# A bias table through 16 copies and 8 skewed loads, a spread scale row, and another opening order

## Chip, cores, metric

The kernel runs on one core of one Trainium2 chip. The metric is the device time of one execution in microseconds (us); of several runs the median counts. Lower is better.

## What is computed

Two layers of a decoder block on 256 rows of width 1024, all in float32. Cut to what matters here:

```python
def hybrid_layer(x, rel_bias, norm1_g, w_in, ...):
    h = rms_norm(x, norm1_g)                 # rows scaled by norm1_g
    z = h @ w_in                             # columns for retention, conv, gMLP, window attention, gates
    ...
    yd = swa_attention(zd, swa_q_g, swa_k_g, swa_sinks, rel_bias)
    ...
    x = x + mix @ w_out                      # mix: the four branches, gated and summed
    h = rms_norm(x, norm2_g)
    return x + swiglu(h)

def swa_attention(...):                      # blocks of 128 rows, window 128, 8 heads
    s = q @ k.T * d ** -0.5
    bias = rel_bias[t5_bucket(dist)]         # a function of the distance and the head alone
    s = where(valid, s + bias, -inf)
    p = softmax with one sink per head
```

The bias of a head depends on the distance alone. So a table of 384 values per head, read with a shift of one place per query row, gives the 128 x 256 block of biases.

## The kernel before

**Tiles.** The 256 rows are two tiles of 128 (t = 0, 1). Weights stream from HBM in units of 1 MB; a unit is two halves of 512 KB (`raw`, 6 buffers). Each half is split in two float32r parts: ScalarE (ACT) rounds it to `wh` (`part`, L117), VectorE (DVE) subtracts to get `wl` (L118); there are 8 buffers of each. A product is three matmuls (`mm`, L140 to L142): xh·wh, xh·wl, xl·wh. Every half gives 12 such matmuls over the two tiles.

**Order of the work in a layer.** `columns` takes the window attention's q columns (4 halves), its k and v columns (2 halves), then, as chunks of 4 halves, the conv input `pa`, the conv gate `pg`, retention q, k, v, gate, and the gMLP. The window attention is a generator (`swa_task`): transposes of q and k (`swa_qkT`) fall due after `pa`, scores and row maxima (`swa_soft`, with the bias added on DVE at L375) after `pg`, the exponentials follow on ACT (L389, L395). Gates, branches, output projection and FFN follow.

**Who sets the order.** Except in the opening, which is written out by hand on TensorE (PE), ACT and DVE, a scheduler places the instructions of each engine. All loads of weights are issued by the SyncE queue (SPq), in order, and so are nearly all other transfers: what waits in that queue holds back every load behind it. Each engine, too, works strictly in its own order.

**Opening and norm.** `opening` loads tile 0 of x, the scale row of the first norm spread to 128 partitions (`load_norm`, L223, 512 KB), and the first 4 halves. PE runs warm-up matmuls on a tile of zeros. `norm` squares and sums on ACT (L198), takes the root on GpSimd (`rsqrt`, L184), scales on DVE (L207); PE transposes, and `split` (ACT L174, DVE L176) makes the two parts of h.

**Bias table.** `constants` builds it, called after the q, k and v columns: a matmul (L281) of the 32 x 8 `rel_bias` with a 32 x 384 table of ones and zeros (`hot`) gives 8 rows of 384; DVE adds the mask (`jm`, L283); one transfer (L285) writes each of the 8 rows 128 times to DRAM (`rd`, 8 x 128 x 384), and one load (L288) reads it back with a row step of 383 elements, so that each partition is shifted by one.

Of the kernel before, what the change touches and what calls it, by code (L numbers as in the profile page):

```python
# [16 lines left out]
P = 128  # L17
D = 1024
# [13 lines left out]
LEAD = 96  # L32
C_QG, C_KG, C_CB, C_LG, C_LB, C_GB, C_SK, C_CW = 0, 1, 2, 6, 10, 14, 18, 26
# [47 lines left out]
class Kernel:  # L81
# [110 lines left out]
    def norm(self, t, raw=False):  # L192
        nc = self.nc
        x, g = self.x[t], self.ng
        ms = self.small("ms")
        hn = [self.work("hn") for _ in range(2)]
        for n in range(2):
            nc.scalar.activation(  # L198
                hn[n], x[:, n * 512 : (n + 1) * 512], AF.Square, scale=1.0 / 32.0, accum_out=ms[:, n : n + 1]
            )  # L200
# [4 lines left out]
        for n in range(2):  # L205
            s = slice(n * 512, (n + 1) * 512)
            nc.vector.scalar_tensor_tensor(  # L207
                out=hn[n], in0=x[:, s], scalar=ms[:, 3:4], in1=g[:, s], op0=ALU.mult, op1=ALU.mult
            )
# [16 lines left out]
    def setup(self):  # L226
# [3 lines left out]
        self.nhalf = self.lead.tile([P, LEAD], F32, name="nhalf")  # L230
        nc.gpsimd.memset(self.nhalf, -0.5)
# [3 lines left out]
    def opening(self):  # L235
        nc, a, pin = self.nc, self.a, self.tc.keep_in_program_order
        self.setup()
        for n in range(2):
            c = slice(n * 512, (n + 1) * 512)
            pin(nc.sync.dma_start(out=self.x[0][:, c], in_=a["x"][0:P, c]))  # L240
        nc.scalar.dma_start(out=self.ident, in_=a["ident"])
        self.ng = self.load_norm(0, 0)
# [3 lines left out]
        self.warm = self.wk.tile([P, W], BF16, tag="wk", name="warm")  # L246
        EN = mybir.EngineType
        with self.tc.manual_schedule(engines={EN.PE, EN.Activation, EN.DVE}):
            nc.vector.memset(self.warm, 0.0)
            self.warm_up(14)  # L250
            hn = self.norm(0, raw=True)
            ps = [self.transpose4(hn[n]) for n in range(2)]
            self.warm_up(3)
            h0 = self.act_tile(0)
            nc.vector.tensor_copy(first[0][0], first[0][2])
            self.split(h0, 0, ps[0], 1.0)
            nc.vector.tensor_tensor(
                out=first[0][1], in0=first[0][2], in1=first[0][0].bitcast(F32), op=ALU.subtract
            )
            self.split(h0, 4, ps[1], 1.0)  # L260
            for half in first[1:]:
                self.part(*half)
        return h0
# [5 lines left out]

    def constants(self):  # L270
        nc, cp, a = self.nc, self.cp, self.a
        c = cp.tile([P, NCONST], F32, name="const")
        self.const = c
        rel = cp.tile([32, 8], F32, name="rel")
        hot = self.wk.tile([32, 384], F32, tag="wk", name="hot")
        jm = self.wk.tile([8, 384], F32, tag="wk", name="jm")
        nc.sync.dma_start(out=rel, in_=a["rel_bias"])
        nc.sync.dma_start(out=hot, in_=a["hot"])
        nc.sync.dma_start(out=jm, in_=a["jmask"])
        ps = self.bank()  # L280
        nc.tensor.matmul(ps[:8, :384], rel, hot, start=True, stop=True)  # L281
        r8 = self.wk.tile([8, 384], F32, tag="wk", name="r8")
        nc.vector.tensor_tensor(out=r8, in0=ps[:8, :384], in1=jm, op=ALU.add)  # L283
# [650 lines left out]
def shape_constants():  # L934
# [26 lines left out]
    jmask = np.tile(np.where(valid, 0.0, NEG).astype(np.float32)[None], (8, 1))  # L961
    return const, hot, jmask, np.eye(P, dtype=np.float32)
# [47 lines left out]
```

## Time and profile before

| what | value |
|---|---|
| median of 3 runs | 980.57 us (980.22 to 982.9) |
| the profiled execution's own time | 982.4 us |
| its span in the profile | 980.3 us |
| busy: PE, DVE, ACT, POOL | 956.2, 681.7, 482.5, 38.7 us |
| HBM read, mean | 175.46 MB, 182 GB/s |

The span is the time from the first to the last instruction that the profiler recorded; the execution's own time is a little longer than that. PE is busy nearly all the time, but a busy share is an average over stages: the 24 us in which PE has nothing to do lie mostly in two places, at the start and some 60 us in. Busy time of PE also holds matmuls that run at the lower of TensorE's two clock levels; the granted clock (PEclk, 1.00 is 2.4 GHz, 0.50 is 1.2 GHz) shows where.

### The profile page before, as it was taken

The page shows a single profiled execution, that of the slowest core. Times are in us where ns is not written, and L with a number is a line of the kernel's source. Part 1 is how long each engine was busy: PE and PEld are TensorE (multiplying, and loading weights), DVE is VectorE, ACT ScalarE, POOL GpSimd, SP SyncE. Part 2 cuts the span into 40 slices and gives each one's busy share as a digit, 9 for nine tenths or more (in the row PEclk, how much of TensorE's full clock was granted, in tenths as well). Part 3 has the DMA queues.
Part 4 walks back from the last instruction along what each step waited for, and adds up shares of the span by engine and source line. Part 5 has one row for each costly group of instructions (what it writes and reads, how often), then busy time and mean ns, then how long its engine had stood idle before and what let it go on. Part 6 is the DMA issues. An engine that isn't in the chain of part 4 may idle for free.

```text
span 980.3 us, 12353 instructions
## 1 busy us (share of the span) xinstructions
PE 956.2 (98%) x4567; PEld 789.3 (81%) x4567; DVE 681.7 (70%) x1051; ACT 482.5 (49%) x688; POOL 38.7 (4%) x38
## 2 busy tenths in 40 slices
PE   8959999999999999999999999999999999999998
PEld 5846788888888888888988778888888888888887
DVE  6507999999767655556566699999866676555552
ACT  5407846454555444444455774644446455444440
POOL 0200001100000000000001000100010000000000
PEclk9988999999999999999999999999999999999999
DMA  9558564665654665655555246466656357656521
GB/s 350 169 79 294 172 231 160 226 198 180 199 166 154 213 221 183 196 184 183 190 171 210 91 155 212 129 192 194 194 176 193 105 191 244 203 177 194 190 89 43
DMA packets 51060, 178.89 MB, mean 182 GB/s; under 512 B 5520, under 2 KB 7992, under 8 KB 50872
## 3 DMA queue, kind: packets, MB, share of 16 engines
q1 hardware_dynamic: 50856, 178.04, 56.1%
q8 instruction: 36, 0.59, 0.2%
q14 instruction: 24, 0.20, 0.1%
q10 hardware_dynamic: 144, 0.07, 0.0%
HBM read 175.46 MB, written 2.62 MB: 182 GB/s over the span
## 4 chain that ended last, share of the span: by engine, by line
PE 90%; DMA 4%; ACT 3%; DVE 2%; issue 1%; SPq 0%; POOL 0%; ACTq 0%; DVEq 0%
PE acc L141 20%; PE acc L142 20%; PE acc L140 20%; PE mid L140 8%; PE mid L142 8%; PE mid L141 8%; DMA raw<-wu 3%; PE mid L167 2%; ACT sc L389 1%; PE mid L817 1%; ACT sc L395 1%; DVE wl L118 1%; DMA ng<-norms 1%; ACT wh L117 0%; PE mid L588 0%
## 5 line engine op out<-in xcount | busy, mean ns | idle before, releaser
L118 DVE TENSOR_TENSOR wl<-raw,wh 128x1024 fp32r<-128x1024 f32 x319 | 385.2, 1223 | 183.4 <-ACT wh L117 178.8
L117 ACT CAST wh<-raw 128x1024 fp32r<-128x1024 f32 x319 | 332.2, 1055 | 314.0 <-PE acc L142 163.7
L140 PE MATMUL acc<-wh,hT 128*128 128x512 f32 (+1 forms) x640 | 250.5, 392 | 13.7 <-ACT wh L117 13.7
L141 PE MATMUL acc<-wl,hT 128*128 128x512 f32 (+1 forms) x640 | 248.0, 387 | 1.0 <-DVE wl L118 0.9
L142 PE MATMUL acc<-wh,hT 128*128 128x512 f32 (+1 forms) x640 | 247.9, 387 | 0.0
L140 PEld LDWEIGHTS acc<-wh,hT 128*128 128x128 f32 x640 | 121.1, 189 | 37.4 <-ACT wh L117 14.1
L140 PE MATMUL mid<-wh,hT 128*128 128x512 f32 (+1 forms) x384 | 143.7, 374 | 0.0
L142 PE MATMUL mid<-wh,hT 128*128 128x512 f32 (+1 forms) x384 | 142.7, 372 | 0.0
L141 PEld LDWEIGHTS acc<-wl,hT 128*128 128x128 f32 x640 | 121.1, 189 | 26.8 <-DVE wl L118 2.8
L141 PE MATMUL mid<-wl,hT 128*128 128x512 f32 (+1 forms) x384 | 142.6, 371 | 0.0
L142 PEld LDWEIGHTS acc<-wh,hT 128*128 128x128 f32 x640 | 120.7, 189 | 25.3 <-issue 0.6
L140 PE MATMUL acc<-wh,yT 128*128 128x512 f32 x304 | 119.1, 392 | 0.0
L141 PE MATMUL acc<-wl,yT 128*128 128x512 f32 x304 | 118.4, 389 | 0.0
L142 PE MATMUL acc<-wh,yT 128*128 128x512 f32 x304 | 118.1, 389 | 0.0
L446 DVE SCALAR_TENSOR_TENSOR ca<-uT,col,ca 128x256 f32<-128x256 f32 x240 | 101.8, 486 | 3.4 <-ACT ca L440 3.3
L142 PEld LDWEIGHTS mid<-wh,hT 128*128 128x128 f32 x384 | 72.3, 188 | 12.6
L140 PEld LDWEIGHTS mid<-wh,hT 128*128 128x128 f32 x384 | 72.3, 188 | 12.2
L141 PEld LDWEIGHTS mid<-wl,hT 128*128 128x128 f32 x384 | 72.4, 188 | 12.2
L142 PEld LDWEIGHTS acc<-wh,yT 128*128 128x128 f32 x304 | 57.1, 188 | 12.2 <-DVE yT L821 0.3
L140 PEld LDWEIGHTS acc<-wh,yT 128*128 128x128 f32 x304 | 57.1, 188 | 11.8 <-ACT yT L820 0.4
L141 PEld LDWEIGHTS acc<-wl,yT 128*128 128x128 f32 x304 | 57.1, 188 | 11.5
L740 ACT ACTIVATE gth<-acc 128x512 f32<-128x512 f32 x32 | 19.2, 599 | 30.9 <-PE acc L142 30.9
(141 smaller groups left out, 590.8 us busy)
## 6 DMA issues: line engine op xcount, KB each, us to landing
raw<-wu SPq DMA_DIRECT2D x320, 512.0 KB, 4.2
ng<-norms SPq DMA_DIRECT2D x4, 512.0 KB, 5.7
rows<-rows SPq DMA_DIRECT2D x2, 768.0 KB, 6.3
rd<-r SPq DMA_DIRECT2D x1, 1536.0 KB
const<-const SPq DMA_DIRECT2D x1, 1088.0 KB, 6.8
bias<-rd SPq DMA_DIRECT2D x1, 1024.0 KB, 5.7
out<-x SPq DMA_DIRECT2D x4, 256.0 KB, 2.0
x<-x SPq DMA_DIRECT2D x2, 256.0 KB, 3.5
```

The source lines that it names most:

```text
L117: nc.scalar.copy(h, src)
L118: nc.vector.tensor_tensor(out=lo, in0=src, in1=h.bitcast(F32), op=ALU.subtract)
L140: nc.tensor.matmul(ps, xh, hs, start=start, stop=False)
L141: nc.tensor.matmul(ps, xh, ls, start=False, stop=False)
L142: nc.tensor.matmul(ps, xl, hs, start=False, stop=stop)
L167: self.nc.tensor.transpose(ps[:, b * P : (b + 1) * P], src[:, b * P : (b + 1) * P], self.ident)
L389: nc.scalar.activation(sc[:, h, :], sc[:, h, :], AF.Exp, bias=nm[:, h : h + 1], accum_out=den[:, h : h + 1])
L395: nc.scalar.activation(sc[:, h, :], sc[:, h, :], AF.Copy, scale=den[:, h : h + 1])
L446: nc.vector.scalar_tensor_tensor(out=self.ca[:, c, :], in0=self.uT[:, c, k : k + T * P], scalar=w[:, c, k : k + 1], in1=self.ca[:, c, :], ...
L740: self.nc.scalar.activation(th[t, n], ps[t], AF.Tanh, scale=0.5)
L817: nc.tensor.transpose(ps[:, b * P : (b + 1) * P], s[t][:, b * P : (b + 1) * P], self.ident)
```

## The change

The table of biases is made otherwise. `hot` gets a 33rd row with the mask, `rel` a 33rd row of ones, and GpSimd makes 16 copies of the 8 columns of `rel` side by side (`wide`). One matmul (33 x 128 by 33 x 384) then gives 128 rows of 384, row 8c + h being copy c of head h, mask included. ACT copies them out of PSUM, one transfer writes them to DRAM (`rd`, now 128 x 384), and 8 loads, each for 16 partitions, read it back skewed. The matmul, copy and write stand at the end of the opening (`bias_rows`), `rel` and `hot` are loaded on ACT's queue at the start, the 8 loads stay in `constants`.

The first norm's scale row is loaded as two rows of 512 on one partition (`grow`) on ACT's queue, and spread by two matmuls with a row of ones into two PSUM banks (`gps`); the first norm reads these, and ACT copies them to `ng` for the second tile's norm. The square and sum of the second half of tile 0 moves from ACT to DVE. Warm-ups, and the order of casts and splits in the opening, change too.

```diff
-    def norm(self, t, raw=False):
+    def norm(self, t, raw=None):
...
+        g = raw or [self.ng[:, n * 512 : (n + 1) * 512] for n in range(2)]
...
+            if raw and n == 1:
+                nc.vector.tensor_tensor_reduce(
+                    out=hn[n], in0=xs, in1=xs, scale=1.0 / D, scalar=0.0,
+                    op0=ALU.mult, op1=ALU.add, accum_out=ms[:, n : n + 1],
+                )
+            else:
+                nc.scalar.activation(hn[n], xs, AF.Square, scale=1.0 / 32.0, accum_out=ms[:, n : n + 1])
...
     def opening(self):
...
+        grow = []
+        for n in range(2):
+            grow.append(self.wk.tile([1, W], F32, tag="wk", name="grow"))
+            nc.scalar.dma_start(out=grow[n], in_=a["norms"][0, 0:1, n * 512 : (n + 1) * 512])
         nc.scalar.dma_start(out=self.ident, in_=a["ident"])
-        self.ng = self.load_norm(0, 0)
+        rel, hot = self.bias_inputs()
         first = self.fetch(0, True) + self.fetch(1, True)
...
-            self.warm_up(14)
-            hn = self.norm(0, raw=True)
-            ps = [self.transpose4(hn[n]) for n in range(2)]
+            self.warm_up(7)
+            gps = [self.abank() for _ in range(2)]
+            for n in range(2):
+                nc.tensor.matmul(gps[n], self.ones, grow[n], start=True, stop=True)
             self.warm_up(3)
+            hn = self.norm(0, raw=gps)
+            for n in range(2):
+                nc.scalar.copy(self.ng[:, n * 512 : (n + 1) * 512], gps[n])
+            ps = []
+            for n in range(2):
+                ps.append(self.transpose4(hn[n]))
+                self.warm_up(1)
+            for half in first[:2]:
+                nc.scalar.copy(half[0], half[2])
             h0 = self.act_tile(0)
-            nc.vector.tensor_copy(first[0][0], first[0][2])
-            self.split(h0, 0, ps[0], 1.0)
...
+            for n in range(2):
+                lows[n]()
+                self.split(h0, 4 * n, ps[n], 1.0)
+            for half in first[2:]:
                 self.part(*half)
+        self.bias_rows(rel, hot)
         return h0
...
+    def bias_inputs(self):
+        nc, cp, a = self.nc, self.cp, self.a
+        rel = cp.tile([REL + 1, 8], F32, name="rel")
+        hot = self.wk.tile([REL + 1, 384], F32, tag="wk", name="hot")
+        nc.gpsimd.memset(rel[REL : REL + 1, :], 1.0)
+        nc.scalar.dma_start(out=rel[0:REL, :], in_=a["rel_bias"])
+        nc.scalar.dma_start(out=hot, in_=a["hot"])
+        return rel, hot
+
+    def bias_rows(self, rel, hot):
+        nc = self.nc
+        wide = self.sm.tile([REL + 1, COPIES, 8], F32, tag="kn", name="wide", bufs=2)
+        nc.gpsimd.tensor_copy(out=wide, in_=rel.unsqueeze(1).broadcast_to([REL + 1, COPIES, 8]))
+        ps = self.bank()
+        nc.tensor.matmul(ps[:, :384], wide.rearrange("p c h -> p (c h)"), hot, start=True, stop=True)
+        r = self.work("r8")
+        nc.scalar.copy(r[:, :384], ps[:, :384])
+        self.rd = self.dr.tile([P, 384], F32, name="rd")
+        nc.sync.dma_start(out=self.rd, in_=r[:, :384])
+
     def constants(self):
...
-        rd = self.dr.tile([8, P, 384], F32, name="rd")
-        nc.sync.dma_start(out=rd, in_=r8.unsqueeze(1).broadcast_to([8, P, 384]))
         self.bias = cp.tile([P, 8, 256], F32, name="bias")
-        skew = bass.AP(rd.tensor, rd.offset + 127, ap=[[383, P], [P * 384, 8], [1, 256]])
-        nc.sync.dma_start(out=self.bias, in_=skew)
-        nc.sync.dma_start(out=c, in_=a["const"])
+        for i in range(P // COPIES):
+            skew = bass.AP(
+                self.rd.tensor, self.rd.offset + 127 - COPIES * i, ap=[[8 * 384 - 1, COPIES], [384, 8], [1, 256]]
+            )
+            nc.sync.dma_start(out=self.bias[COPIES * i : COPIES * (i + 1)], in_=skew)
+        self.const = cp.tile([P, NCONST], F32, name="const")
+        nc.sync.dma_start(out=self.const, in_=a["const"])
```

The edit moves work that it does not name, because the scheduler places everything behind the opening anew. Two places matter.

The SyncE queue of the kernel before, from the x tile on (x_91 is tile 1 of x; each `raw` is a half of a weight unit):

```order
L245 DMA x_91<-x 128x1024
L108 DMA raw<-wu 128x1024 x6
L294 DMA col<-cols 128x150
L277 DMA rel<-rel_bias 32x8
L289 DMA const<-const 128x2176
L108 DMA raw<-wu 128x1024 x4
L308 DMA rows<-rows 128x1536
L278 DMA hot<-hot 32x384
L279 DMA jm<-jmask 8x384
L310 DMA ws<-wsT 128x512
L108 DMA raw<-wu 128x1024 x2
L285 DMA rd<-r_382 1024x1x384
```

The same place in the changed kernel:

```order
L258 DMA x_91<-x 128x1024
L109 DMA raw<-wu 128x1024 x2
L332 DMA col<-cols 128x150
L327 DMA const<-const 128x2176
L109 DMA raw<-wu 128x1024 x2
L316 DMA rd<-r_192 128x384
L109 DMA raw<-wu 128x1024 x2
L325 DMA bias<-rd 16x8x256 x8
L109 DMA raw<-wu 128x1024 x4
```

With the 4 halves ahead of these rows, the write of `rd` has moved from behind 16 halves to behind 8, and the skewed loads from behind 18 halves to behind 10; the constants load now stands ahead of the seventh half instead of the eleventh.

DVE of the kernel before, from the row table on (swqn and kn are the normed q and k, skT the transposed k, cvu the conv branch's input):

```order
L283 TENSOR_TENSOR r_382<-mid,jm 8x384
L118 TENSOR_TENSOR wl<-raw,wh 128x1024
L351 TENSOR_SCALAR skT<-mid,derived 128x128
L118 TENSOR_TENSOR wl<-raw,wh 128x1024
L351 TENSOR_SCALAR skT<-mid,derived 128x128
L426 SCALAR_TENSOR_TENSOR cvu<-cvth,acc 128x512 x2
L118 TENSOR_TENSOR wl<-raw,wh 128x1024 x2
L375 ISA sc,mx<-mid,bias 128x128
L375 ISA mx 128x1
```

DVE of the changed kernel there; of the pairs at L413 that follow one another for tile 0's eight heads the first stands:

```order
L389 TENSOR_SCALAR skT<-mid,derived 128x128 x2
L413 ISA sc,mx<-mid,bias 128x128
L413 ISA mx 128x1
...
L420 TENSOR_TENSOR mx<-mx,col 128x8
L421 TENSOR_SCALAR nm<-mx 128x8
L423 TENSOR_TENSOR es<-col,mx 128x8
L413 ISA sc,mx<-mid,bias 128x256
L413 ISA mx 128x1
L119 TENSOR_TENSOR wl<-raw,wh 128x1024
```

The additions that need the bias came after the `wl` of 18 halves; now they stand directly behind skT, after the `wl` of 10 halves, and ahead of the eleventh. On PE the scores have moved in the same way, from behind `pg` to ahead of it.

## Rows read from the trace of the kernel before

**Rows 1.** The page: busy time, and the two splitting steps of the weights

```profile
PE 956.2 (98%) x4567; PEld 789.3 (81%) x4567; DVE 681.7 (70%) x1051; ACT 482.5 (49%) x688; POOL 38.7 (4%) x38
...
L118 DVE TENSOR_TENSOR wl<-raw,wh 128x1024 fp32r<-128x1024 f32 x319 | 385.2, 1223 | 183.4 <-ACT wh L117 178.8
L117 ACT CAST wh<-raw 128x1024 fp32r<-128x1024 f32 x319 | 332.2, 1055 | 314.0 <-PE acc L142 163.7
```

**Rows 2.** Windows: stretch and length, busy us of each engine, PEclk, DMA share, GB/s

```profile
44.01:115.74 71.73, 56.63 (x276) 43.12 (x275) 36.30 (x90) 38.18 (x87) 0.00 (x0) 0.90 0.59 162
61.93:75.63 13.70, 0.00 (x1) 0.01 (x1) 0.03 (x1) 1.05 (x1) 0.00 (x0) 0.69 0.50 91
75.63:80.90 5.27, 5.23 (x12) 3.69 (x13) 4.21 (x18) 1.72 (x2) 0.00 (x0) 0.51 1.06 401
...
534.57:590.00 55.43, 54.16 (x277) 42.46 (x277) 41.22 (x99) 38.74 (x88) 0.00 (x0) 1.00 0.42 142
```

**Rows 3.** The chain that ended last, first 130 us: start, us, what

```profile
1.64 6.39 DMA ng<-norms
...
38.57 0.74 PE mid L281 x2
...
41.58 32.93 DMA raw<-wu
```

**Rows 4.** Timeline of the SyncE queue: start, us, issues merged over the stretch

```profile
26.72 1.69 SPq L108 DMA_DIRECT2D raw<-wu  x2
40.67 0.81 SPq L285 DMA_DIRECT2D rd<-r  x1
41.58 14.04 SPq L108 DMA_DIRECT2D raw<-wu  x2
73.26 0.39 SPq L288 DMA_DIRECT2D bias<-rd  x1
```

**Rows 5.** Waits of the SyncE queue: us in total, times, longest

```profile
SPq L288 <- DMA rd<-r: 17.6, 1, 17.6
```

**Rows 6.** DMA issues: count, KB each, median us from issue to landing

```profile
raw<-wu SPq DMA_DIRECT2D x320, 512.0 KB, 4.2
...
rd<-r SPq DMA_DIRECT2D x1, 1536.0 KB
...
bias<-rd SPq DMA_DIRECT2D x1, 1024.0 KB, 5.7
out<-x SPq DMA_DIRECT2D x4, 256.0 KB, 2.0
...
hot<-hot SPq DMA_DIRECT2D x1, 48.0 KB, 8.1
```

**Rows 7.** Windows, while `rd` is being written

```profile
45.00:50.00 5.00, 5.00 (x23) 4.13 (x22) 0.49 (x2) 0.00 (x0) 0.00 (x0) 1.00 0.45 52
```

**Rows 8.** Timeline of the opening

```profile
1.17 5.40 PE L268 MATMUL mid<-warm 128*128 128x512 bf16 x14 [1.17 <-DVE warm L249]
...
5.89 0.55 POOL L184 TENSOR_TENSOR ms<-ms,nhalf 128x1 f32<-128x1 f32 x1 [4.86 <-DVE ms L201]
...
8.17 1.42 DVE L207 SCALAR_TENSOR_TENSOR hn<-x,ms,ng 128x512 f32<-128x512 f32 x2 [2.43 <-DMA ng<-norms]
...
11.61 0.99 PE L140 MATMUL acc<-wh,hT 128*128 128x512 f32 x1
```

**Rows 9.** Timeline at the transposes of q and k, layer 1

```profile
43.00 0.60 PE L167 MATMUL mid<-ident,swqn 128*128 128x128 f32 x4
...
43.64 1.14 ACT L350 COPY swqT<-mid 128x512 f32<-128x512 f32 x2 [3.81 <-PE mid L167]
```

**Rows 10.** Timeline at the scores of layer 2, where the bias has long been there

```profile
545.41 1.16 PE L368 MATMUL mid<-skT,swqT 64*128 64x128 f32 x16
547.21 2.20 PE L368 MATMUL mid<-skT,swqT 64*128 64x256 f32 x16 [0.63 <-DVE mx L375]
...
546.44 0.28 DVE L375 CUSTOM_DVE_ANT_0 sc<-mid,bias 128x128 f32<-128x128 f32 x1
```

More of the change, by code (lines that the diff above doesn't have):

```diff
@@ L207, in norm @@
             nc.vector.scalar_tensor_tensor(
-                out=hn[n], in0=x[:, s], scalar=ms[:, 3:4], in1=g[:, s], op0=ALU.mult, op1=ALU.mult
+                out=hn[n], in0=x[:, s], scalar=ms[:, 3:4], in1=g[n], op0=ALU.mult, op1=ALU.mult
             )
@@ L230, in setup @@
         self.nhalf = self.lead.tile([P, LEAD], F32, name="nhalf")
+        self.ones = self.sm.tile([1, P], F32, tag="jk", name="ones", bufs=1)
+        nc.gpsimd.memset(self.ones, 1.0)
         nc.gpsimd.memset(self.nhalf, -0.5)
@@ L246, in opening @@
         self.warm = self.wk.tile([P, W], BF16, tag="wk", name="warm")
+        self.ng = self.cp.tile([P, D], F32, tag="ng", name="ng")
         EN = mybir.EngineType
@@ L249, in opening @@
             nc.vector.memset(self.warm, 0.0)
-            self.warm_up(14)
-            hn = self.norm(0, raw=True)
-            ps = [self.transpose4(hn[n]) for n in range(2)]
+            self.warm_up(7)
+            gps = [self.abank() for _ in range(2)]
+            for n in range(2):
+                nc.tensor.matmul(gps[n], self.ones, grow[n], start=True, stop=True)
             self.warm_up(3)
-            h0 = self.act_tile(0)
-            nc.vector.tensor_copy(first[0][0], first[0][2])
-            self.split(h0, 0, ps[0], 1.0)
[L257 to L261, printed above, removed]
+            hn = self.norm(0, raw=gps)
[7 more added lines that the diff above has]
+                nc.scalar.copy(half[0], half[2])
+            h0 = self.act_tile(0)
+            lows = [
+                lambda i=i: nc.vector.tensor_tensor(
+                    out=first[i][1], in0=first[i][2], in1=first[i][0].bitcast(F32), op=ALU.subtract
+                )
+                for i in range(2)
+            ]
+            for n in range(2):
+                lows[n]()
+                self.split(h0, 4 * n, ps[n], 1.0)
+            for half in first[2:]:
                 self.part(*half)
+        self.bias_rows(rel, hot)
         return h0
@@ L270, in constants @@
     def constants(self):
         nc, cp, a = self.nc, self.cp, self.a
[L272 to L280, printed above, removed]
@@ L960, in shape_constants @@
     hot = ((np.arange(32)[:, None] == bucket[None, :]) & valid[None, :]).astype(np.float32)
-    jmask = np.tile(np.where(valid, 0.0, NEG).astype(np.float32)[None], (8, 1))
-    return const, hot, jmask, np.eye(P, dtype=np.float32)
+    hot = np.concatenate([hot, np.where(valid, 0.0, NEG).astype(np.float32)[None]], 0)
+    return const, hot, np.eye(P, dtype=np.float32)
 def kernel(**inputs):
@@ L989 @@
     cols[:, :, C_CW:] = cw.reshape(L, P, 4 * TAPS)
-    const, hot, jmask, ident = shape_constants()
+    const, hot, ident = shape_constants()
     arrays = {
@@ L998 @@
         "rel_bias": np.ascontiguousarray(i["rel_bias"]),
-        "const": const, "hot": hot, "jmask": jmask, "ident": ident,
+        "const": const, "hot": hot, "ident": ident,
     }
```

11 lines of the change are left out of this document (4 added, 7 removed).

## Prediction

> **What bounds the kernel now.** I read the page first: PE is busy for 956.2 of 980.3 us [rows 1], so whatever time can be won lies in the 24.1 us without a matmul and in stretches at the lower clock. Then the windows. From 61.93 to 75.63 no engine does anything: 13.70 us with one PE instruction and ACT busy for 1.05 us at its very end. Behind it, from 75.63 to 80.90, PE has work but the granted clock is 0.51, the lower of its two levels (1.2 GHz), after 13.7 us of idleness [rows 2]. The chain of waits says what ended last there: a load of weights, 32.93 us long [rows 3]. The transfer itself is not slow (4.2 us from issue to landing is usual [rows 6]); it was issued late. The timeline of the SyncE queue shows why: two halves are issued by 28.4, then nothing until the write of `rd` at 40.67 (it waits for the row table); two halves follow, and then the queue stands before the skewed load of `bias` until 73.26, having waited 17.6 us for that write to land [rows 4, 5]. All later weights stand behind it. The write moves 1536 KB [rows 6] in 73.26 - 40.67 = 32.6 us, 47 to 48 GB/s, and while it runs alone 0.45 of the 16 DMA engines is busy [rows 7]. So in this stage the bound is neither PE nor DMA bandwidth but one transfer, and a queue that waits for it.
>
> How much that costs can be checked against layer 2, which does the same work with the bias at hand. From the end of the transposes of q and k, layer 1 needs 71.73 us for 276 PE instructions, layer 2 needs 55.43 us for 277 [rows 2]: some 16.5 us more. The stall (13.70) and half of the slow stretch (5.27 x (1 - 0.51) = 2.6) make 16.3 of it.
>
> **The change, part by part.**
>
> *Write of rd.* 128 rows of 384 floats, 197 KB instead of 1536 KB. At the old rate, the upper bound, that is 4.1 us; the stores of the output, 256 KB from 128 partitions in 2.0 us, give the lower [rows 6]. The latter is the nearer shape (one row from each partition). It is issued once ACT has copied the rows out of PSUM, at about 14 us by my sum of the opening below; with loads queued ahead of it I take it as landed at 20.
>
> *Eight skewed loads for one.* The same 1 MB. The queue takes some 0.4 us for each issue (0.39 for the one before [rows 4]), 3.3 us together; if they overlap, the last lands within 5.7 us of its issue, as the whole table did [rows 6]: 20 + 3.3 + 5.7 = 29. The reader on DVE is due at about 45: transposes end at 44.01 before [rows 2], copies and first scores follow. So 16 us are in hand, and the four halves behind the loads, at 4.2 us each, overlapped, are there by 35 to 40, while `pg` needs the first at 44. This covers both bounds of the write. Against the change speaks a rule of the Trainium skill (DMA: Bandwidth & Descriptors, section Bandwidth): batch transfers to 1 MiB or more, since each has a fixed part; by its fit, 2.0 us plus bytes over 436 GB/s, eight loads of 131 KB strictly in a row would take an estimated 18.4 us. By that estimate the bias lands at 20 + 18.4 = 38.4, some 6 us ahead of its reader instead of 16: the sum stays, and the rival of late loads gains by it. No row of this trace shows such loads in a row.
>
> *The stall goes:* -13.7. *The half-speed stretch goes with it:* -2.6.
>
> *What is late next.* The new order puts the additions of the bias directly behind skT on DVE and the eleventh half's `wl` behind nine of them; PE has only two matmuls of `pg` to run meanwhile. Counted from the end of the transposes: the first copy of q arrives 0.2 us later (it ends 43.64 + 0.6, the transposes at 44.01 [rows 9]); PE makes tile 0's scores in 1.16 us and DVE adds at 0.21 us a head (it starts 0.3 after the first half of the scores), so done at about 2.7; three small DVE steps 0.3, one addition for tile 1 0.35, `wl` 1.22 [rows 1], done at 4.6. PE's own work in that time is 1.16 + 7/8 of 2.20 [rows 10] + 2 x 0.23 = 3.5, so it stands still for about 1.1 us. Against this, layer 1's stretch has 71.73 - 56.63 - 13.70 = 1.4 us of PE idleness outside the stall [rows 2], behind it, where ACT had the exponentials of both tiles and the delayed casts at once; I take half of that off. Net +0.4. Bounds: 0 (layer 2 waits 0.63 us at this place [rows 10]) and +3 (nothing of the old idleness goes, and the second `wl` is late too). ACT has the exponentials and 12 casts of 1.05 us [rows 1] to do between 44 and 69, about 25 us of work, and PE needs these casts over 33 us: it is not the next bound.
>
> *Opening, the scale row.* The 512 KB load took 6.39 us and ended last there; DVE's scaling waited 2.43 us for it [rows 3, 8]. Now two matmuls of 512 columns with a row of ones: the nearest row is the old table product, 384 columns in 0.74 [rows 3], so 0.74 x 512 / 384 = 1.0 us each, twice that at the lower clock. Seven warm-ups take 7 x 5.40/14 = 2.7 to 3.0 us from 1.17, so the two end at about 5.9 and 6.8. The second half of the squares runs on DVE beside ACT, so the root on GpSimd can start at about 5.4 instead of 5.89 [rows 8], and scaling at 6.4 and 7.1 instead of 8.17: 1.7 us earlier.
>
> *Opening, what gives it back.* ACT now has two copies of `ng` (0.6 each, as a copy of 512 columns [rows 9]) and two casts (1.05 each) ahead of the two splits; one of these casts was on DVE. The splits come at about 10.5, the first product at 11.2 instead of 11.61 [rows 8]. Tile 0's q columns then end 0.9 us earlier, but ACT's copy of the bias rows (0.5 us) and four casts now stand ahead of tile 1's split, and three `wl` ahead of its DVE part: tile 1's products start about 0.7 us later than before. The old table product (0.74 [rows 3]) is gone from the middle of `pa`; the new one is covered by PE's wait for the first split. Together -1.0 by the transposes of q and k. Bounds: -2 (the casts wait for nothing and clock and `wl` keep up) and +3. The latter from a wait that is new: on GpSimd the copies of `rel` (`wide`) stand ahead of the first norm's root, and behind that root DVE's scaling, PE's transposes and ACT's copies all wait. `rel` is issued fourth on ACT's queue, at about 2.1 (0.4 us an issue from 0.7 on); if it took the 8.1 us of `hot` [rows 6], the root would start at 10.6 and scaling at 11.4, 3.2 us later than before. I take 2 to 2.5 us for it, since that row was issued behind megabytes of weights on its own queue, and `rel` is not.
>
> *Nothing else:* the mask addition on DVE (one step), GpSimd's copies and the two memsets lie in time when these engines idle, as their 70% and 4% show [rows 1]; if that cover failed, each is below 1 us. The rest of the program keeps its order on PE.
>
> **Sum.** -13.7 - 2.6 + 0.4 - 1.0 = -16.9. The profiled execution took 982.4 us by its own time, 2.1 over its span; 982.4 - 16.9 = 965.5. It lies 1.8 above the median of the runs shown (980.57); against the median the forecast is 963.7.
>
> **Rivals.**
> 1. *The new order, or late loads, hold PE at the start of `pg`.* Everything behind the additions on DVE waits for the last of eight loads. If they land at 48 to 50 instead of 29 (each of the eight taking about 3.5 us in a row), PE loses 3 to 6 us more: 967 to 970. For it: the loads share their queue with weights and the eighth waits for the ninth and tenth half. Against: 16 us in hand. Chance 0.12.
> 2. *The opening loses what it should win*, by `rel` late on GpSimd or by ACT's longer row of steps: +2 to +3 instead of -1.0, so 966.7 to 967.7. For it: ACT's part of the opening grows by some 3 us. Chance 0.12.
> 3. *Slower than before.* If the loads from DRAM cannot overlap and each takes the 5.7 us that the old single load took [rows 6], the last lands at 20 + 8 x 5.7 = 66. DVE then stands before its first addition until 66, and with it the eleventh half; PE stands from about 45 on, 21 us, longer than the old stall, and the clock falls again: 963.7 + 21 + 2.6 = 987. It decides the sign from a landing at about 59 on. Against: two 512 KB loads are issued within 1.69 us [rows 4], though one lands after 4.2 [rows 6], so loads do overlap; and the old 5.7 was for eight times the bytes. Chance 0.03. The Trainium skill (DMA: Bandwidth & Descriptors, section Anatomy of one DMA) lays the fixed part to waiting for completion rather than to setting up, which speaks for overlap too; no row here shows it for small loads.
> 4. *The change does not free the stage*, since the small write lands as late as the large one (something else makes it slow): about 980. Against: 0.45 of the DMA engines was busy for the whole time, so it was moving bytes. Chance 0.02.
>
> **Numbers.** My forecast has a chance of 0.71; its own range is 961 to 967. With rivals 1 and 2 the range is 960.5 to 970; what is left out is rivals 3 and 4 and the far ends of the bounds. A measurement of this kernel can tell about 0.3% (3 us) from no change: faster 0.95, same 0.02, slower 0.03.
>
> **What would show it.** Right: no gap in PE between 60 and 76, PEclk 1.00 from the opening on, the eight loads landed before 35, a PE gap of 1 to 2 us behind the transposes of q and k, the SyncE queue no longer waiting for `rd` for more than about 6 us, and the first product at about 11. Wrong: DVE's first addition waiting for `bias`, GpSimd's copy waiting for `rel` beyond 5 us, or the gap at `pg` above 3 us.

## The result, and the profile after

The changed kernel takes 966.6 us (966.35 to 967.12, 4 runs), the kernel before 980.6 (980.22 to 982.9, 4 runs): ratio 0.9853, interval 0.9836 to 0.987. It is faster by 14 us; 963.7 was forecast, and 966.6 lies inside the range. The profiled execution took 966.61 with a span of 964.5, so from span to span the change is 980.3 - 964.5 = 15.8 us, where the sum of the prediction said 16.9. (The medians and ratios below leave out one slow execution of 1950.94 us, of the run e6.)

The windows of both kernels, cut at the same two places: from the second set of transposes of layer 1's normed q and k to the first retention score. First the kernel before, then the changed one (stretch and length, busy us of PE, PEld, DVE, ACT, POOL, then PEclk, DMA share, GB/s).

```profile
43.55:134.67 91.12, 76.02 (x363) 59.19 (x362) 55.49 (x119) 49.26 (x99) 0.00 (x0) 0.93 0.62 180
```

```profile
44.52:118.88 74.36, 73.89 (x364) 58.55 (x363) 65.35 (x132) 54.83 (x105) 0.00 (x0) 1.00 0.61 202
60.00:76.00 16.00, 16.00 (x80) 12.98 (x80) 13.63 (x26) 13.91 (x34) 0.00 (x0) 1.00 0.74 241
8.00:18.00 10.00, 9.21 (x24) 6.19 (x25) 8.10 (x10) 9.16 (x15) 2.54 (x4) 0.50 1.02 418
```

The stretch in which everything stood [rows 2] is now full of matmuls at full clock. PE's idle time in this stage was 91.12 - 76.02 = 15.10 us and is 74.36 - 73.89 = 0.47; its busy time fell by 2.13 us, for the same matmuls, since none runs at the lower level any more (PEclk 1.00 for 0.93). Together 16.76. Behind the first retention score nothing changed: 980.3 - 134.67 = 845.6 us then, 964.5 - 118.88 = 845.6 now. That leaves the opening: the transposes started at 43.55 and now start at 44.52, so it became 0.97 us **longer**, and -16.76 + 0.97 is the 15.8 of the spans. The last row shows one thing about it: from 8 to 18 us PE ran at a granted clock of 0.50, the lower level.

The SyncE queue of the changed kernel (start, us, issues), and what the view of the tile `bias` says of its eight loads, from issue to landing:

```profile
15.18 0.33 SPq L316 DMA_DIRECT2D rd<-r  x1
20.91 4.21 SPq L325 DMA_DIRECT2D bias<-rd  x8
```

```profile
DMA to landing us min/median/max: 5.0/6.6/7.2
```

The write is issued at 15.18 instead of 40.67 and has landed before 20.91; it took 32.6 us before [rows 4]. The eight loads are issued by 25.1 and, at 7.2 us at most, have landed by about 32. Their reader, DVE's first addition, runs at 46.0 and waits for PE, not for them. They overlapped and needed about 11 us together. The estimate of 18.4 for eight loads strictly in a row, from the Trainium skill's fit of 2.0 us plus bytes over 436 GB/s (DMA: Bandwidth & Descriptors, section Anatomy of one DMA; a fit for transfers that GpSimd issues, these are issued by SyncE), did not price them.

What PE waits for in the whole program (us in total, times, longest):

```profile
PE mid L168 <- DVE hn L214: 1.8, 1, 1.8
...
PE acc L142 <- DVE wl L119: 0.2, 1, 0.2
```

The longest is at the very start; the `wl` of the eleventh half, for which a wait of about a microsecond was forecast, cost 0.2. The timeline of the opening (start, us, what, in brackets the idle time before it and what ended it), to be read against rows 8 and 9:

```profile
1.95 0.45 ACTq L303 DMA_DIRECT2D rel<-rel_bias  x1
...
4.27 2.02 PE L267 MATMUL acc<-grow,ones 1*128 1x512 f32 x4
...
7.07 0.28 POOL L310 COPY wide<-rel 33x128 f32<-33x128 f32 x1 [5.74 <-DMA rel<-rel_bias]
7.40 0.55 POOL L185 TENSOR_TENSOR ms<-ms,nhalf 128x1 f32<-128x1 f32 x1
7.99 1.40 DVE L214 SCALAR_TENSOR_TENSOR hn<-x,ms,acc 128x512 f32<-128x512 f32 x2 [2.56 <-POOL ms L185]
...
13.12 0.79 PE L141 MATMUL acc<-wh,hT 128*128 128x512 f32 x1
...
43.98 0.60 PE L168 MATMUL mid<-ident,swqn 128*128 128x128 f32 x4
```

The scale row is no longer late: the products with ones run at 4.27. But GpSimd's copy `wide` stands ahead of the root and waited 5.74 us for `rel`. The root ran at 7.40 (5.89 before [rows 8]), the scaling at 7.99 (8.17 before), and, with one more cast and two copies on ACT ahead of the splits, the first product came at 13.12 instead of 11.61.

### The profile page after: what moved, and what is told of

It reads as the page before. It is cut to its first block, busy times and chain, and to the rows that moved or that the text cites. A ratio compares the mean times of both kernels' runs of the same rounds, so it can differ in the third digit from the quotient of the medians.

```text
span 964.5 us, 12359 instructions
## 1 busy us (share of the span) xinstructions
PE 956.0 (99%) x4566; PEld 790.6 (82%) x4566; DVE 681.5 (71%) x1051; ACT 483.3 (50%) x690; POOL 38.0 (4%) x41
## 4 chain that ended last, share of the span: by engine, by line
PE 96%; ACT 1%; DVE 1%; DMA 1%; issue 0%; ACTq 0%; POOL 0%; DVEq 0%; POOLq 0%
PE acc L143 22%; PE acc L142 22%; PE acc L141 22%; PE mid L143 8%; PE mid L141 8%; PE mid L142 8%; PE mid L168 2%; PE mid L855 1%; ACT sc L427 1%; PE mid L454 1%; DMA rel<-rel_bias 1%; PE mid L443 0%; PE mid L626 0%; DVE wl L119 0%; PE mid L574 0%; DVE sc L413 0%
```

## The experiments

Three sessions, e1 to e4, e5 to e8 and e9 to e12, each on another chip; the kernel before took 981.74, 982.47 and 981.46 us (medians of 13, 7 and 9 runs) in them, so ratios are given. (e5 and e11 ran on different chips, other than e11's expectation says.) None leaves out any part of the computation. Two readings of each profile sort the runs: when the second transposes of q and k start (the opening), and how long it is from there to the first retention score (the stage). The rest was 845.5 to 845.7 us in all fourteen profiles, so these two make the whole difference. The last column says how many of the 16 additions of the bias stand on DVE ahead of the next low part `wl`, and on ACT how many exponentials stand ahead of the next cast.

| kernel | opening | stage | span | median, ratio | additions, exponentials ahead |
|---|---|---|---|---|---|
| before | 43.55 | 91.12 | 980.3 | 980.6 | other order |
| changed | 44.52 | 74.36 | 964.5 | 966.6, 0.9853 | 9, 0 |
| e1 table only | 43.82 | 84.18 | 973.6 | 975.6, 0.9942 | 16, 7 |
| e2 opening only | 42.73 | 89.81 | 978.2 | 980.4, 0.9985 | other order |
| e3 `wide` behind root | 41.91 | 85.38 | 972.8 | 975.5, 0.9939 | 16, 7 |
| e4 and copies late | 44.40 | 84.69 | 974.7 | 976.7, 0.9949 | 13, 7 |
| e5 e3, const early | 42.66 | 75.44 | 963.6 | 965.7, 0.9838 | 8, 0 |
| e6 e1, const early | 44.35 | 75.44 | 965.4 | 966.3, 0.9849 | 8, 0 |
| e7 rel first | 45.51 | 75.41 | 966.5 | 968.2, 0.9861 | 8, 0 |
| e8 1536 KB, 128 rows | 43.37 | 75.43 | 964.3 | 967.0, 0.9854 | 8, 0 |
| e9 bias product early | 43.84 | 75.43 | 964.9 | 966.8, 0.9848 | 8, 0 |
| e10 rel before ident | 43.43 | 74.31 | 963.3 | 965.8, 0.9838 | 9, 0 |
| e11 changed again | 44.42 | 74.32 | 964.4 | 966.5, 0.9844 | 9, 0 |
| e12 e5 again | 41.69 | 75.45 | 962.8 | 965.0, 0.9833 | 8, 0 |

### e1: the table alone

The opening of the kernel before, with `bias_inputs`, `bias_rows` and the eight loads of the change.

```diff
-            self.warm_up(7)
-            gps = [self.abank() for _ in range(2)]
...
-            hn = self.norm(0, raw=gps)
+            self.warm_up(14)
+            hn = self.norm(0, raw=True)
```

> The opening of the kernel before (scale row loaded by one transfer to 128 partitions, 14 warm-ups, both squares on ScalarE), with the new bias table (16 copies, small write, 8 skewed loads). Theory A: the table alone brings the whole gain and the new opening costs about 1 us of it; then the transposes of q and k end at about 44.0 us in as before (45.0 in the changed kernel) and the median is 964 to 966, the upper end if the scheduler puts all 16 additions of the bias ahead of the next weight split. Rival: the new opening is worth something to the gain; then the median is above 967 and the transposes end later than 45.

975.61 us, ratio 0.9942 (0.9927 to 0.9956): a miss by some 10 us. The stall is gone, but PE has two new waits in the stage (waits of PE in e1, then the stage's window):

```profile
PE acc L141 <- ACT cvth L437: 3.9, 1, 3.9
PE acc L141 <- ACT wh L118: 3.1, 1, 3.1
```

```profile
43.82:128.00 84.18, 76.31 (x364) 60.77 (x363) 73.26 (x150) 55.77 (x105) 0.00 (x0) 0.96 0.54 178
```

### e2: the opening alone

The changed opening, with the table of the kernel before, built in `constants`.

```diff
-        rel, hot = self.bias_inputs()
...
-        self.bias_rows(rel, hot)
```

> The new opening with the old bias table (8 rows, each written 128 times, one skewed load); GpSimd has no copies of rel ahead of the first norm's root. Theory A: the stall of some 13 us is back, 978 to 982. Theory rel: the root on GpSimd starts at about 5.4 instead of 7.4 and the transposes of q and k end at 42.5 to 43.5 instead of 45.0. Theory ACT (ScalarE's longer row of copies and casts sets the opening): they end at about 45 in spite of the early root.

980.36 us, ratio 0.9985 (0.9976 to 0.9994). The root runs at 5.65, the first product at 10.70, and the transposes are 0.82 us earlier than before: here, without `wide` on GpSimd, the opening does what was forecast of it. The stage is nearly as long as it was, 89.81 for 91.12.

### e3: `wide` behind the root

```diff
-        nc.gpsimd.tensor_copy(out=wide, in_=rel.unsqueeze(1).broadcast_to([REL + 1, COPIES, 8]))
+        self.tc.keep_in_program_order(
+            nc.gpsimd.tensor_copy(out=wide, in_=rel.unsqueeze(1).broadcast_to([REL + 1, COPIES, 8]))
+        )
```

(and the first norm's root likewise, so that it stays ahead)

> The changed kernel with GpSimd's 16 copies of rel held behind the first norm's root. Theory rel: the root starts at about 5.4 instead of 7.4, scaling at about 6.4 instead of 8.0, first product at about 11.2 instead of 13.1, the transposes of q and k end at about 43 instead of 45, so 1.5 to 2 us off the median (965) unless the scheduler's new order behind gives it back. Theory ACT or clock: the transposes still end at 44.5 to 45.

975.49 us, ratio 0.9939 (0.9924 to 0.9954). The opening followed the theory: root at 5.92, first product at 10.99, transposes 2.6 us earlier than in the changed kernel. But the stage grew by 11 us. The scheduler had placed what stands behind the opening anew. ACT of e3, at the first exponential and the next cast:

```profile
45.60 0.40 ACT L431 ACTIVATE sc<-sc,nm 128x128 f32<-128x128 f32 x1 [2.47 <-DVE nm L425]
...
48.40 1.03 ACT L118 CAST wh<-raw 128x1024 fp32r<-128x1024 f32 x1
```

ACT of the changed kernel, at the same place:

```profile
45.65 1.05 ACT L118 CAST wh<-raw 128x1024 fp32r<-128x1024 f32 x1
48.22 0.40 ACT L427 ACTIVATE sc<-sc,nm 128x128 f32<-128x128 f32 x1 [1.52 <-DVE nm L421]
```

In the changed kernel ACT makes the cast while it would otherwise wait for DVE's maxima; in e3 it idles 2.47 us, then does seven exponentials, and the cast ends at 49.4. The bias is not late there: DVE's first addition, at 43.38, waits 0.38 us for PE. PE, which has no weights left, stands 3.13 us before it, and again 3.16 us at 67 for the conv gate's step on ACT (PE's timeline in e3, then the stage's window):

```profile
49.48 1.22 PE L141 MATMUL acc<-wh,hT 128*128 128x512 f32 x2 [3.13 <-ACT wh L118]
...
67.01 0.80 PE L141 MATMUL acc<-wh,hT 128*128 128x512 f32 x1 [3.16 <-ACT cvth L466]
```

```profile
41.91:127.29 85.38, 78.76 (x364) 62.44 (x363) 73.29 (x150) 55.77 (x105) 0.00 (x0) 0.92 0.54 177
```

6.62 us of the stage are idle (85.38 - 78.76), against 0.47; the other part is matmuls at the lower clock behind these waits (78.76 busy against 73.89).

### e4: e3, and ACT's copies of `ng` later

```diff
             hn = self.norm(0, raw=gps)
-            for n in range(2):
-                nc.scalar.copy(self.ng[:, n * 512 : (n + 1) * 512], gps[n])
...
             for half in first[2:]:
                 self.part(*half)
+            for n in range(2):
+                nc.scalar.copy(self.ng[:, n * 512 : (n + 1) * 512], gps[n])
```

> As the run with the copies of rel behind the root, and ScalarE's two copies of the scale row to ng moved behind the first four casts. Theory ACT: the two splits come 1.2 us earlier, and so do the first product (about 10) and the transposes of q and k. Theory clock: PE runs at the lower level then anyway and the transposes end within 0.5 us of that run.

976.72 us, ratio 0.9949 (0.9932 to 0.9965). The products with ones took 3.77 us here and 2.14 in e3, the first product came at 13.50, and until 16.7 the products run at the lower level (last section), so the comparison says nothing clear on the copies. The stage again has the late casts.

### e5 and e6: the order alone

To test the order by itself, `const` (1088 KB) is loaded ahead of the skewed loads; nothing else is moved by hand.

```diff
+        self.const = cp.tile([P, NCONST], F32, name="const")
+        nc.sync.dma_start(out=self.const, in_=a["const"])
         self.bias = cp.tile([P, 8, 256], F32, name="bias")
...
-        self.const = cp.tile([P, NCONST], F32, name="const")
-        nc.sync.dma_start(out=self.const, in_=a["const"])
```

> The kernel of e3_wide_behind_root (GpSimd's copy `wide` behind the first norm's root) with one line moved: the load of `const` is written ahead of the eight skewed loads. By it the order on VectorE and ScalarE behind the transposes of the window's q and k is again an interleaved one: 8 additions, then two low parts of weights, and one cast ahead of the first exponential; in e3_wide_behind_root all 16 additions and seven exponentials stand ahead of the next cast. Theory 'order' (e3_wide_behind_root lost because VectorE and ScalarE did the softmax ahead of the casts and low parts that TensorE needs next): from the end of those transposes to the first retention score it takes about 74 us, as in the changed kernel, not the 84.9 of e3_wide_behind_root; the opening stays as in that run (root by 6, transposes at about 41.4); span about 962, time 963 to 965, so faster than the changed kernel's 966.6 by 2 to 3. Rival 'bias late' (the loss came with late bias or weight loads, not with the order): the stage stays near 85 us and the time near 975.

> The kernel of e1_table_only (opening of before, new bias table) with the same one line moved, so that its order behind the transposes of q and k is interleaved too. Theory 'order': from the end of those transposes (about 44 us) to the first retention score about 74 us, not 84.2; time 965 to 966.5, so the bias table alone brings all that the change brings, and the new opening nothing. Rival 'the opening makes the stage': near 975.6, as e1_table_only.

e5: 965.74 us, ratio 0.9838 (0.982 to 0.9855), a little above what was expected (963 to 965), as the opening took 42.66 and the stage 75.44. e6: 966.28, ratio 0.9849 (0.9829 to 0.987). Both stages are 75.44 us, 9.9 and 8.7 less than in e3 and e1. The load itself is not it: `const` is issued at 22.9 in e3 and at 17.5 in e5, first read by GpSimd at 37.5 and 39.6, and the waits of PE that went were for ACT's cast and gate step, which stood behind tile 0's exponentials and tile 1's softmax and not behind a transfer. So the order is what cost e1 and e3 their 10 us, and the table alone, with a good order, brings all that the change brings (e6 966.3, changed 966.6). The stage's window of e6:

```profile
44.35:119.79 75.44, 74.32 (x363) 58.41 (x362) 67.13 (x136) 54.98 (x105) 0.00 (x0) 1.00 0.59 200
```

The remaining 1.1 us to the changed kernel's 74.36 come in every run with eight additions ahead (75.41 to 75.45), in none with nine (74.31 to 74.36): 0.65 more idle, as PE waits 0.8 us for `wl` instead of 0.2, and 0.43 more busy.

### e7: `rel` first

```diff
+        rel, hot = self.bias_inputs()
         grow = []
...
         nc.scalar.dma_start(out=self.ident, in_=a["ident"])
-        rel, hot = self.bias_inputs()
+        nc.scalar.dma_start(out=hot, in_=a["hot"])
...
-        nc.scalar.dma_start(out=hot, in_=a["hot"])
```

> The changed kernel with the load of `rel` (1 KB) first on ScalarE's queue, ahead of the two halves of the norm's scale row and of `ident`, and `hot` behind them. Theory (the root waits behind `wide`, which waits for `rel`): `rel` lands by about 4, `wide` runs by 4 to 5.3, the root at 5.3 to 6 in place of 7.40, the scaling at 6 to 6.5, the transposes of q and k at 42 to 43 in place of 43.98; time 964 to 965.6. Rival (products with ones or the scaling become late by the two rows loaded later, or the weights' first halves set the first product): root early, but transposes of q and k within 0.3 of 43.98 and the time 966.3 to 967.

968.21 us, ratio 0.9861 (0.9839 to 0.9882): a miss. The start did what was expected (timeline of e7), the end did not:

```profile
3.32 0.28 POOL L310 COPY wide<-rel 33x128 f32<-33x128 f32 x1 [1.99 <-DMA rel<-rel_bias]
...
5.19 0.56 POOL L185 TENSOR_TENSOR ms<-ms,nhalf 128x1 f32<-128x1 f32 x1 [1.59 <-DVE ms L208]
...
24.72 0.56 PE L143 MATMUL acc<-wh,hT 128*128 128x512 f32 x1 [2.06 <-DVE hT L177]
```

`rel` landed before 3.32, the root ran at 5.19 and the first product at 11.90. But by the chain of waits a half of the weights took 9.23 us to land, until 19.33:

```profile
10.10 9.23 DMA raw<-wu
```

Its `wl` stands on DVE ahead of tile 1's split, PE waited 2.06 us for that split, and the granted clock fell to 0.63 for the four microseconds from 24. The first product was 1.2 us earlier than in the changed kernel and the transposes 1.0 later. The stage has the order of e5, 75.41.

### e8: the old number of bytes, from 128 rows

```diff
-        self.rd = self.dr.tile([P, 384], F32, name="rd")
-        nc.sync.dma_start(out=self.rd, in_=r[:, :384])
+        self.rd = self.dr.tile([P, 8, 384], F32, name="rd")
+        nc.sync.dma_start(out=self.rd, in_=r[:, :384].unsqueeze(1).broadcast_to([P, 8, 384]))
...
-                self.rd.tensor, self.rd.offset + 127 - COPIES * i, ap=[[8 * 384 - 1, COPIES], [384, 8], [1, 256]]
+                self.rd.tensor, self.rd.offset + 384 * i + 127 - COPIES * i, ap=[[64 * 384 - 1, COPIES], [8 * 384, 8], [1, 256]]
```

> The changed kernel, but the write of the bias rows again writes 1536 KB: each of the 128 rows (16 copies of 8 heads) is written eight times, and each of the eight skewed loads reads its own repeat. Theory 'bytes' (the write of before was long because it wrote 1536 KB): at before's 47 to 52 GB/s it takes about 30 us again, the skewed loads are issued at 45 or later, land at 50 or later, and TensorE stalls for 5 us or more between 50 and 75; time 975 or more. Theory 'rows' (it was long because its bytes left 8 rows of SBUF, and 128 rows use all 16 DMA engines where 8 rows showed a share of 0.45): the write lands within 14 to 20 us of its issue at about 15, the skewed loads are issued by about 36, no stall over 3 us; time 967 to 972, the loss being weights that come later.

967.04 us, ratio 0.9854 (0.9836 to 0.9872), the changed kernel's ratio; the write landed sooner than either theory said. The queue of e8, and the window of its write:

```profile
15.36 0.60 SPq L316 DMA_DIRECT2D rd<-r  x1
24.03 4.58 SPq L325 DMA_DIRECT2D bias<-rd  x8
```

```profile
15.40:24.00 8.60, 8.16 (x51) 6.92 (x49) 8.49 (x10) 6.89 (x12) 2.67 (x4) 1.00 1.03 406
```

The same 1536 KB that took 32.6 us from 8 rows [rows 4] take at most 8.7 us from 128 rows, and that beside weights that fill all DMA engines. So not the bytes made the old write slow but the 8 rows of SBUF that it read: with them 0.45 of the DMA engines was busy [rows 7]. The Trainium skill has the rule (DMA: Bandwidth & Descriptors, section Why a DMA increments its semaphore by 16 and not by 1): a transfer runs on the largest number of engines, up to 16, that divides the outermost sizes of its two patterns, so 8 for 8 rows and 16 for 128. The share of 0.45 and this run agree with it. But the number of engines is not all: half of them would take twice as long, and the old write took at least 3.7 times as long. By its window each busy engine moved 52 / (0.45 x 16) = 7 GB/s [rows 7], in e8's window, weights included, 406 / (1.03 x 16) = 25. What held each engine back with 8 rows is not shown by any run. The prediction took the bytes for the cause in its upper bound (4.1 us at the old rate) and the shape only in its lower one; the bytes did not matter.

### e9: the bias product ahead

```diff
-            self.warm_up(3)
             hn = self.norm(0, raw=gps)
+            bps = self.bias_product(rel, hot)
...
             for half in first[2:]:
                 self.part(*half)
-        self.bias_rows(rel, hot)
+            r = self.work("r8")
+            nc.scalar.copy(r[:, :384], bps[:, :384])
+        self.bias_rows(r)
```

> The kernel of e5_root_first_const_early, with TensorE's product for the bias rows moved from in front of the first product with weights (11.93, 1.05 us there) to the place of three warm-ups behind the products with ones; its copy on ScalarE and the write keep their places. The order on VectorE, ScalarE and SP is that of e5. Theory 'weights' (from about 8 us on the DMA engines are full at 400 GB/s and more, so the weights' arrival and not the first product sets when the transposes of q and k are done): first product 0.5 to 1.1 earlier than 12.91, but those transposes less than 0.4 earlier than 42.66 and the time within 0.5 of that of e5 in the same session. Theory 'one to one' (what the prediction assumed: an opening shorter by x brings the whole kernel x): transposes and time earlier by as much as the first product, so the time 0.5 to 1.1 below e5.

966.78 us, ratio 0.9848 (0.9835 to 0.9862), 1.8 us above e5's kernel in the same session (e12, 964.95). The step that was to be shortened grew: `hot` was not there (timeline of e9).

```profile
8.98 1.62 PE L318 MATMUL mid<-hot,wide 33*128 33x384 f32 x2 [2.73 <-DMA hot<-hot]
```

PE stood 2.73 us with nothing else allowed ahead, the first product came at 12.79 instead of e12's 10.86, and the transposes 2.15 us later. It does not tell the two theories apart as planned, but a delay of 1.9 us at the first product did come through whole.

### e10 to e12: `rel` one place earlier, and both kernels in one session

e10, against the changed kernel:

```diff
-        nc.scalar.dma_start(out=self.ident, in_=a["ident"])
         rel, hot = self.bias_inputs()
+        nc.scalar.dma_start(out=self.ident, in_=a["ident"])
+        nc.scalar.dma_start(out=hot, in_=a["hot"])
...
-        nc.scalar.dma_start(out=hot, in_=a["hot"])
```

> The changed kernel with the load of `rel` one place earlier on ScalarE's queue, ahead of `ident`, so about 0.4 earlier and ahead of the first weights; the orders on VectorE, ScalarE and SP stay those of the changed kernel, to the row. Theory (root waits behind `wide`, `wide` for `rel`): `rel` lands by 4 to 5.5, the root runs at 5.3 to 6, the scaling at 6 to 6.6; the transposes of the first norm then wait for `ident` (issued at about 2, landed at about 8, as in e7_rel_first) and start at about 8.1 in place of 8.79; transposes of q and k 0.3 to 0.7 earlier than 43.98; stage behind them 74.4 as in the changed kernel; time 0.3 to 0.7 below the changed kernel in the same session. Rival (first product does not matter): same time as the changed kernel within 0.3.

> The changed kernel once more, on the chip of e5 and e9, so that they can be compared in one session. 966.6 as before, within 0.6; ratio to the kernel before 0.985. From the end of the transposes of q and k to the first retention score 74.4, by the order theory.

> The kernel of e5_root_first_const_early once more, in one session with the changed kernel. If its opening is really better (first norm's root not behind `rel`), it is 0.5 to 1.5 below the changed kernel: 965.1 to 966.1 where that gives 966.6. If the difference of 0.9 between the two sessions was the chip, the two are the same within 0.4.

e10 965.80 us (0.9838, 0.9824 to 0.9851), e11 966.54 (0.9844, 0.983 to 0.9858), e12 964.95 (0.9833, 0.9819 to 0.9846). GpSimd and DVE at the first norm, in e10, in e11 and in e12, and e12's window of the stage:

```profile
6.64 0.28 POOL L310 COPY wide<-rel 33x128 f32<-33x128 f32 x1 [5.32 <-DMA rel<-rel_bias]
```

```profile
8.27 0.28 POOL L310 COPY wide<-rel 33x128 f32<-33x128 f32 x1 [6.94 <-DMA rel<-rel_bias]
```

```profile
5.58 0.55 POOL L185 TENSOR_TENSOR ms<-ms,nhalf 128x1 f32<-128x1 f32 x1 [4.25 <-DVE ms L210]
6.17 1.41 DVE L216 SCALAR_TENSOR_TENSOR hn<-x,ms,acc 128x512 f32<-128x512 f32 x2 [0.74 <-POOL ms L185]
...
7.37 0.28 POOL L313 COPY wide<-rel 33x128 f32<-33x128 f32 x1 [1.23 <-DMA rel<-rel_bias]
```

```profile
41.69:117.14 75.45, 74.33 (x364) 58.42 (x363) 67.16 (x136) 55.00 (x105) 0.00 (x0) 1.00 0.61 200
```

`rel` lands between 6.6 and 8.2 us in these three runs, and only e12's root does not wait for it. In e10 it was expected by 4 to 5.5; issued one place earlier, at 1.52, it was hardly sooner than in the changed kernel (`wide` at 6.64 for 7.07). e10, with the orders of the changed kernel, has transposes 0.99 us earlier and the same stage as e11; its median is 0.7 lower, though the intervals overlap, and the unchanged opening alone was profiled between 43.37 (e8) and 44.52. e12 has transposes 2.73 us earlier, gives 1.13 back through its order, and ends 1.6 lower in span and in median; here too the intervals of the ratios still overlap, but its highest run (965.86) lies below the changed kernel's median in both its sessions, and two of e11's five runs (965.02, 965.31) fall among its own. It has the lowest median of this study. Its opening with the order of nine additions would by the same sum give a span of 41.69 + 74.32 + 845.65 = 961.7; this was not built.

## Why the prediction was right, and where it was not

**The stall: right, and for 0.9 us more than it said.** Stage term -13.7 - 2.6 + 0.4 = -15.9, measured -16.76. The idle part was to fall by 13.3 and fell by 14.6: the new wait behind the transposes of q and k was 0.5 us and not 1.1 (PE waits 0.27 and 0.18 there, and ACT had made a cast before the exponentials), and all of the old idleness of 1.4 went, not half. The clock's part was 2.13 for 2.6. (Layer 1's surplus over layer 2, from which the check of these terms starts, is 71.73 - 55.43 = 16.3 and not 16.5.)

**The opening: longer than forecast in every profile of it.** -1.0 was forecast. The changed opening was profiled three times: +0.97, +0.87 in e11, and -0.18 in e8, which up to there differs only in the bytes of its write. The step that failed is "I take 2 to 2.5 us for it, since that row was issued behind megabytes of weights on its own queue, and `rel` is not". `rel` took 5.0 us from its issue (5.2 in e8, 6.2 in e11): it has its own queue, but four halves of weights are issued from 1.64 on, ahead of its 1.95, and move over the same DMA engines; issued at 0.72, ahead of them, it landed before 3.32 (e7). To stand just ahead is not enough: in e10 it was issued 0.1 us before the first of them and took 5 us too. The Trainium skill states the rule (DMA: Bandwidth & Descriptors, section Issuing engines are not separate DMA queues): transfers that different engines issue run on the same 16 DMA engines and interleave; 5.0 against at most 2.6 us for this 1 KB agrees with it. The bound that was kept for it, the 8.1 us of `hot`, held. Rival 2 named this mechanism; it came true, but at no more than +0.97 instead of +2 to +3. e2, e3, e5 and e12, whose root does not wait for `rel`, give -0.82, -1.64, -0.89 and -1.86, so without that one wait the term would have been about right; e4, without it too, gives +0.85, with its products at the lower level until 16.7. That level is the second thing the term left out: in the changed kernel's profile the first products start 0.43 us apart until 18.0, in e8 0.23 apart from the first on, and e8's transposes are 1.15 us earlier though its root is 0.18 later. How the +0.97 divides between the two is not shown. One part of the sum does not follow either: tile 0's q columns were to end 0.9 us earlier, but by the prediction's own first product (11.2 for 11.61) it is 0.4, and the term about -0.4.

**The level.** The profiled execution of before was 1.8 us above the median of its runs and I took that off; the changed kernel's lies at its median. By its own time the forecast was 965.5 and came out at 966.61: 1.1 short, the two errors above (-0.9 + 2.0), so the nearness is in part that they cancel. In the later sessions the kernel before had medians of 981.5 to 982.5, so the 980.57 was on the low side.

**The marks.** Right: no gap between 60 and 76, loads landed by about 32 (35), 3.3 us of the queue's wait for `rd` (6), first addition not waiting for `bias`. Wrong: the first product at 13.12 (11), full clock from the opening on (0.50 until 18), and the gap behind the transposes (0.45 us for 1 to 2). GpSimd's copy waited beyond 5 us, which the text had named among the signs of being wrong.

**What was missing.** Rival 1 names the new order, but its price is that of late loads; no rival priced the order of DVE and ACT in the stage by itself, and that had the largest price of all: the same table costs or saves 10 us with it. The forecast used the order that was printed, so it was right; what hid there was how little moves it. e1 (another opening) and e3 (one GpSimd copy behind another) were enough, and one load written two lines earlier put it back.

**Open.** How much of a shorter opening comes through. From e5 to e12, one kernel in two sessions, the first product is 2.05 us earlier and the transposes 0.97. There the lower level took the lead: e12's products run at it until 14.4, e5's do not, and at the tenth product (14.71 and 15.09) it is down to 0.38. In e7 the gain turned into a loss; in e9 a delay came through whole. From 8 to 36 us the windows of these runs, four us each, show a DMA share of 0.9 or more, so the arrival of weights is a likely brake beside it, but no run isolates it.

## What to carry to other kernels

When a scheduler places the rest, price the order and not only the edit: after removing a wait, look at what the engines do first with the work that has become ready, since 16 additions and seven exponentials ahead of the next weight cast cost 10 of 16 us here, and compare any variant at the same two marks before believing its time. A tiny load counts when a small step on the critical chain stands behind its reader on another engine: put the reader behind that step, or the load ahead of the big transfers. Before shrinking a slow transfer look at how many rows it leaves from: with 8 rows under half of the DMA engines were busy, each at a third of the rate or less, and eight times the bytes from 128 rows cost nothing that the ratios show.

## What was not expected of the hardware

The four matmuls with the row of ones took 1.98 to 2.31 us in seven profiles (the changed kernel, e2, e3, e7, e9, e10, e12) and 3.77 or 3.78 in four (e4, e5, e8, e11), though the program up to there is nearly the same and PEclk reads 1.00 over both. Where they were fast, a stretch at about half the clock followed. Where they were slow, PEclk shows none, but the matmuls do: the three warm-ups behind the products took 1.46 us instead of 0.82, and what follows runs at that pace until about 12 us in e5, e8 and e11, in e4 until 16.7 (there 0.63 us for a product, as the changed kernel's at 0.50, and 0.39 in e5). So both kinds have a stretch at the lower level, at different times, and PEclk misses the one of the slow kind. Windows of e12 and of e5:

```profile
8.00:15.00 7.00, 6.87 (x18) 4.19 (x17) 5.39 (x6) 6.88 (x13) 0.00 (x0) 0.53 1.03 420
```

```profile
4.00:15.00 11.00, 11.00 (x29) 5.67 (x29) 6.76 (x10) 7.56 (x13) 0.84 (x2) 1.00 1.00 381
```

The three warm-ups of e12 and of e5, the second product of e4 and of e5, and e4's window from 14 us:

```profile
6.18 0.82 PE L298 MATMUL mid<-warm 128*128 128x512 bf16 x3
7.98 1.46 PE L298 MATMUL mid<-warm 128*128 128x512 bf16 x3
```

```profile
14.10 0.63 PE L142 MATMUL acc<-wl,hT 128*128 128x512 f32 x1
13.25 0.39 PE L142 MATMUL acc<-wl,hT 128*128 128x512 f32 x1
```

```profile
14.00:16.00 2.00, 2.00 (x6) 1.52 (x6) 1.65 (x2) 2.00 (x7) 0.00 (x0) 1.00 0.51 209
```

In the time the two are about 1 us apart: of e5's and e12's four runs each, all one kernel, those with a mean clock of 1.000 took 965.7 to 965.9 and those below it 964.5 to 965.0, so a mean of 1.000 is no sign of a faster run. What decides between the two is not shown by any run.
